# Row sums spread into the attention tile's free half, own slots for the down weights, an early Silu table and fewer warm-ups in a hybrid decoder layer

## The chip, the cores and the metric

One core of a Trainium2 chip runs the whole kernel, one launch. The metric is device time in microseconds (us), lower is better. The kernel before took 1362.46 us (median of 3 runs, 1359.22 to 1362.53). Engines: PE (TensorE), DVE (VectorE), ACT (ScalarE), POOL (GpSimd), SP (SyncE, which here only issues DMAs).

## What is computed

One decoder layer on 16 meta tokens and 1024 tokens of width 1024, in float32:

```python
u = rmsnorm(h, attn_norm_w)
proj = u @ w_in                       # split: gated-DeltaNet heads | forgetting-attention heads
o_gdn = gated_deltanet_group(...)     # 4 heads, chunked delta rule
o_fox = forgetting_attention_group(...)   # 8 heads of 64, softmax attention with a forget-gate bias
h = h + concat(o_gdn, o_fox) @ w_out
h = h + swiglu(rmsnorm(h, ffn_norm_w), w_gate, w_up, w_down)   # (silu(x@w_gate) * (x@w_up)) @ w_down
out = rmsnorm(h, final_norm_w)[16:]
```

The hidden width of the FFN is 2816, that is 22 blocks of 128.

## The kernel before

The stages follow each other on PE: projections and DeltaNet preparation (to about 300 us), scan and remaining projections, attention (to about 610 us), output projection and norm (to about 716 us), first FFN half (to about 1110 us), second FFN half. Every fp32 product is three matmuls: each operand is cut into a rounded high part (`split`, line 158, an ACT cast) and the rest (line 159, a DVE subtraction). In the FFN both products use seven products of sums of quarter blocks instead of eight products (a Strassen scheme, p1 to p7).

PE's order is written out by hand from the scan on (`manual_schedule`); the other engines and the SP queue are put in order by a scheduler that plays the program through with planned durations, so an edit anywhere can exchange neighbours in their queues. Each engine works through its queue in order, SP its DMAs too, and a tile's buffer can be written again only when its last readers are done.

**The attention part of the output projection.** `prep(tt)` (lines 1100 to 1109) readies one of eight token tiles; the order is 0, 4, 1, 5, 2, 6, 3, 7 (`ORDER`). It loads the unnormalised attention output from DRAM into `of` (128 x 8 x 128; the two halves hold the two parts of a split product, two buffers), POOL adds the halves into `of[:, 0:4]` (line 1104), `row_scale` (lines 1091 to 1097) has POOL spread the inverse row sums into a tile `rx` (line 1093), PE transposes `rx` into PSUM (`rbt`, line 1096), DVE multiplies (line 1106), and the product is split into `oh`, `ol`. The tile `rx` has no memory of its own: it lies in the slot `ub0_0`.

That slot belongs to `u_blocks` (lines 1171 to 1204), which transposes the normed tile `xn` (`u2t`, line 1178) and, for tiles 4 to 7, forms the sums for the Strassen scheme; `ub0_0` holds `b12` there, written at line 1196 and read at line 1199. So `rx` of a later tile can be written only after `u_blocks` of an earlier one has read `b12`. `out_fox` (lines 1156 to 1168) does the projection itself, 24 matmuls a tile (`wof`), the residual add on DVE (line 1162), the norm and a store.

**The first FFN half.** `ffn_in(j)` runs 11 pairs of hidden blocks. `w_ops` (lines 1218 to 1230) loads two gate blocks and two up blocks (`raw`, 512 KB each, DMA line 1215), DVE forms four sums for each of gate and up (lines 1223 to 1226), and ACT and DVE split them. `down_sums(j)` (lines 1240 to 1251) loads two blocks of `w_down` into tiles of the same tag `raw` (four buffers for six tiles a pair), POOL forms four sums (lines 1246 to 1249), and four DMAs write them to DRAM (line 1251, `wt_p`). Evictions on DVE are line 1282 (`gx`, `gz` and the like). The split of p1 and p2 of pair 0 is made early, in a pool `pf` (inside `if i == 3`), while the output projection still runs.

At the start 24 matmuls on a tile of ones (`WARM`, line 131) keep PE busy until the first transposes.

Of the kernel before, what the change touches and what calls it, by code (L numbers as in the profile page):

```python
# [9 lines left out]
F32 = mybir.dt.float32  # L10
F32R = mybir.dt.float32r
AF = mybir.ActivationFunctionType
ALU = mybir.AluOpType
# [23 lines left out]
CO = 3.0  # L37
RES = 6
ORDER = (0, 4, 1, 5, 2, 6, 3, 7)
WARM = 24  # L40


class PeOrder:
# [52 lines left out]
def tile_hymba_layer(ctx, tc, x, meta, attn_norm_w, w_in, conv_w, a_log, dt_bias, gdn_norm_w,  # L96
# [991 lines left out]
        turn[tag] = turn.get(tag, -1) + 1  # L1088
        return wo2.tile(shape, dt, tag=slot or f"{tag}_{turn[tag] % bufs}", name=f"{tag}_{nm}")

    def row_scale(tt):
        rx = wo_tile("rx", [P, 4, P], 1, tt, slot="ub0_0")
        G.tensor_copy(rx.rearrange("p m (i c) -> p (m i) c", i=2), rinv[:, :, tt:tt + 1].broadcast_to([P, FH, DH]))
        pt = ps_s(f"rbt_{tt}").rearrange("p (a b) -> p a b", a=4)
        for m in range(4):
            nc.tensor.transpose(pt[:, m], rx[:, m], ident)
        rbk[tt] = pt

    def prep(tt):
        cols = slice(P * tt, P * tt + P)  # L1100
        oh, ol = (wo_tile(t, [P, 4, P], 2, tt, F32R) for t in ("oh", "ol"))
        of = wo_tile("of", [P, 8, P], 2, tt)
        nc.sync.dma_start(of, o_d[:, :, :, cols].rearrange("i k p c -> p (i k) c"))
        G.tensor_tensor(of[:, 0:4], of[:, 0:4], of[:, 4:8], op=ALU.add)
        row_scale(tt)
        V.tensor_mul(of[:, 0:4], rbk[tt], of[:, 0:4])
        cast = split(oh, ol, of[:, 0:4])
        pre_u[tt] = (oh, ol)
        return cast

    def load_h(tt):
# [91 lines left out]
        put("p5", t1, G)  # L1203
        put("p4", t4, G)

    f1 = [None]
    wops = {(m, j): {} for m in "gu" for j in range(NF)}

    def w_split(m, j, p, src, pool, bufs):
        hi, lo = (pool.tile([P, H], F32R, tag=f"w{c}", bufs=bufs, name=f"w{c}_{m}{j}_{p}") for c in "hl")  # L1210
        split(hi, lo, src)
        wops[m, j][p] = (hi, lo)

    def w_raw(t, v, f):
        nc.sync.dma_start(t.rearrange("p (k c) -> p k c", k=KT), v[:, :, P * f:P * f + P])

    def w_ops(v, j, m):
        r0, r1 = (f1[0].tile([P, D], F32, tag="raw", bufs=4, name=f"raw_{m}{j}_{i}") for i in range(2))
        for r, f in ((r0, j), (r1, j + NF)):
            w_raw(r, v, f)  # L1220
        a11, a12, a21, a22 = r0[:, :H], r0[:, H:], r1[:, :H], r1[:, H:]
        s2, s3, s4 = (f1[0].tile([P, H], F32, tag=f"ws{i}", bufs=2, name=f"ws{i}_{m}{j}") for i in range(3))
        V.tensor_tensor(s3, a11, a21, op=ALU.subtract)  # L1223
        V.tensor_tensor(a21, a21, a22, op=ALU.add)
        V.tensor_tensor(s2, a21, a11, op=ALU.subtract)
        V.tensor_tensor(s4, a12, s2, op=ALU.subtract)
        for p, src in zip(ORD, (a11, s2, a12, s3, a21, a22, s4)):
            if p not in wops[m, j]:
                w_split(m, j, p, src, f1[0], 7)
            yield  # L1230

    def block3(dst, p, wop, first):
# [5 lines left out]
                                 stop=(k == 3 and i == 2), skip_group_check=not first)  # L1238

    def down_sums(j):  # L1240
        q0, q1 = (f1[0].tile([P, D], F32, tag="raw", bufs=4, name=f"raw_d{j}_{i}") for i in range(2))
        for q, f in ((q0, j), (q1, j + NF)):
            nc.sync.dma_start(q, w_down[P * f:P * f + P])
        b11, b12, b21, b22 = q0[:, :H], q0[:, H:], q1[:, :H], q1[:, H:]
        t3 = f1[0].tile([P, H], F32, tag="dt3", bufs=1, name=f"dt3_{j}")
        G.tensor_tensor(t3, b22, b12, op=ALU.subtract)
        G.tensor_tensor(b12, b12, b11, op=ALU.subtract)
        G.tensor_tensor(b22, b22, b12, op=ALU.subtract)
        G.tensor_tensor(b21, b21, b22, op=ALU.subtract)
        for p, t in (("p7", t3), ("p5", b12), ("p6", b22), ("p4", b21)):  # L1250
            nc.sync.dma_start(wt_d[p, j], t)
# [59 lines left out]
    with tc.manual_schedule(engines={mybir.EngineType.PE}):  # L1311
# [4 lines left out]
        for i, tt in enumerate(ORDER):  # L1316
            out_fox(tt, 0)
            if i >= 2:
                u_blocks(ORDER[i - 2])
            if i == NT - 1:  # L1320
                u_blocks(ORDER[i - 1])
            out_fox(tt, 1)
            if i + 2 < NT:
                prep(ORDER[i + 2])
                load_h(ORDER[i + 2])
            if i == 3:
                for m, v in (("g", w_g_v), ("u", w_u_v)):
                    r = wraw.tile([P, WMAX], F32, tag="raw", name=f"raw_{m}")[:, :D]
                    w_raw(r, v, 0)
                    for p, src in (("p1", r[:, :H]), ("p2", r[:, H:])):  # L1330
                        w_split(m, 0, p, src, pfp, 4)
        done = [("p1", "g"), ("p1", "u")]
        for p, m in done:
            sbs[m, 0] = {"x": pfp.tile([P, H], F32, name=f"{m}x0")}
# [150 lines left out]
```

## Time and profile before

| | |
|---|---|
| median of 3 runs (range) | 1362.46 us (1359.22 to 1362.53) |
| the profiled execution: its own time, its span | 1361.58 us, 1359.8 us |
| mean granted TensorE clock | 0.986 |
| PE busy | 1308.9 us, 96% of the span |
| DVE, ACT, POOL busy | 859.9, 543.6, 424.0 us |
| HBM traffic | 177 GB/s over the span |

The span runs from the first to the last instruction; the execution's own time is 1.8 us longer. Busy PE time counts a matmul from start to end, also while the granted clock is halved: the share of the full clock has to be read beside it. In rows of the timeline the first number is the start in us from the span's beginning, the second the duration, and brackets hold the idle time of the engine before the instruction and what ended it.

### The profile page before, as it was taken

The page shows a single profiled execution, that of the slowest core. Times are in us where ns is not written, and L with a number is a line of the kernel's source. Part 1 is how long each engine was busy: PE and PEld are TensorE (multiplying, and loading weights), DVE is VectorE, ACT ScalarE, POOL GpSimd, SP SyncE. Part 2 cuts the span into 40 slices and gives each one's busy share as a digit, 9 for nine tenths or more (in the row PEclk, how much of TensorE's full clock was granted, in tenths as well). Part 3 has the DMA queues.
Part 4 walks back from the last instruction along what each step waited for, and adds up shares of the span by engine and source line. Part 5 has one row for each costly group of instructions (what it writes and reads, how often), then busy time and mean ns, then how long its engine had stood idle before and what let it go on. Part 6 is the DMA issues. An engine that isn't in the chain of part 4 may idle for free.

```text
span 1359.8 us, 20162 instructions
## 1 busy us (share of the span) xinstructions
PE 1308.9 (96%) x7417; PEld 1137.2 (84%) x7417; DVE 859.9 (63%) x1505; ACT 543.6 (40%) x914; POOL 424.0 (31%) x422
## 2 busy tenths in 40 slices
PE   8999999999999899999778999999999999999997
PEld 7999999899999778887566878787888888888876
DVE  6565779657446578985677556666555566455653
ACT  6443543222223467872353233222223334333341
POOL 3111123211112256742432444433444443010300
PEclk9999999899999999999898999999999999999998
DMA  8131465784397898836526544445455556965522
GB/s 291 65 91 47 141 178 162 205 229 140 126 314 244 206 260 245 219 98 200 171 93 178 178 152 147 141 155 162 142 170 178 163 179 233 402 246 182 214 84 93
DMA packets 196201, 242.11 MB, mean 178 GB/s; under 512 B 18944, under 2 KB 146808, under 8 KB 192264
## 3 DMA queue, kind: packets, MB, share of 16 engines
q1 hardware_dynamic: 196104, 240.84, 56.6%
q8 instruction: 58, 0.95, 0.3%
q14 instruction: 39, 0.32, 0.1%
HBM read 161.62 MB, written 79.18 MB: 177 GB/s over the span
## 4 chain that ended last, share of the span: by engine, by line
PE 56%; DMA 15%; DVE 14%; POOL 7%; issue 5%; SPq 1%; ACT 1%; DVEq 0%; POOLq 0%; ACTq 0%
PE xp L1395 8%; PE yp L1395 6%; DMA raw_u<-in_w_up_dram 5%; PE pj_fk L199 3%; PE pj_fq L199 3%; DMA wt_p<-raw_d 3%; DMA raw_d<-in_w_down_dram 2%; PE wog L199 2%; PE pt L961 2%; DVE wl_u_p L159 2%; PE po L982 1%; PE pj_k L190 1%; PE pj_k L189 1%; PE pj_v L191 1%; PE pj_q L191 1%
## 5 line engine op out<-in xcount | busy, mean ns | idle before, releaser
L159 DVE TENSOR_TENSOR al_p<-ra_p,ah_p 128x2048 fp32r<-128x2048 f32 (+1 forms) x21 | 46.8, 2230 | 92.5 <-ACT ah_p L158 92.5
L914 POOL TENSOR_TENSOR bi<-ccol,cr 128x144 f32<-128x144 f32 (+7 forms) x60 | 70.7, 1182 | 55.5 <-DVE sm L930 51.2
L158 ACT CAST ah_p<-ra_p 128x2048 fp32r<-128x2048 f32 (+1 forms) x21 | 37.1, 1765 | 103.7 <-PE yp L1395 44.4
L1287 POOL TENSOR_TENSOR gz<-gz,uz 128x512 f32<-128x512 f32 x11 | 18.3, 1665 | 178.9 <-DVE uz L1282 149.8
L1395 PE MATMUL xp<-wl_p,ah_p 128*128 128x512 f32 x176 | 69.3, 394 | 1.8 <-DVE wl_p L159 1.8
L1395 PE MATMUL xp<-wh_p,al_p 128*128 128x512 f32 x176 | 69.1, 393 | 0.0
L1395 PE MATMUL xp<-wh_p,ah_p 128*128 128x512 f32 x176 | 69.0, 392 | 0.0
L158 ACT CAST wh_u_p<-raw_u 128x512 fp32r<-128x512 f32 x44 | 27.2, 620 | 74.6 <-DMA raw_u<-in_w_up_dram 23.7
L159 DVE TENSOR_TENSOR wl_u_p<-raw_u,wh_u_p 128x512 fp32r<-128x512 f32 x44 | 47.0, 1069 | 15.4 <-ACT wh_u_p L158 15.4
L935 ACT ACTIVATE pr<-pr,sm 128x144 f32<-128x144 f32 (+3 forms) x64 | 50.6, 791 | 13.7 <-DVE sm L930 12.1
L159 DVE TENSOR_TENSOR pl<-pt,ph 128x512 fp32r<-128x512 f32 (+1 forms) x96 | 51.5, 552 | 5.1 <-ACT ph L158 4.7
L159 DVE TENSOR_TENSOR wl_g_p<-raw_g,wh_g_p 128x512 fp32r<-128x512 f32 x44 | 38.7, 881 | 23.4 <-ACT wh_g_p L158 23.4
L158 ACT CAST ph<-pt 128x512 fp32r<-128x512 f32 (+1 forms) x96 | 45.2, 473 | 20.3 <-PE pt L961 18.3
L158 ACT CAST wh_g_p<-raw_g 128x512 fp32r<-128x512 f32 x44 | 27.1, 619 | 63.7 <-PE ub L1237 42.0
L1223 DVE TENSOR_TENSOR ws_g<-raw_g,raw_g 128x512 f32<-128x512 f32 x11 | 7.6, 692 | 69.6 <-DMA raw_g<-in_w_gate_dram 69.6
L1395 PE MATMUL yp<-wh_p,ah_p 128*128 128x512 f32 x132 | 51.3, 389 | 0.0
L1395 PE MATMUL yp<-wl_p,ah_p 128*128 128x512 f32 x132 | 51.3, 389 | 0.0
L1395 PE MATMUL yp<-wh_p,al_p 128*128 128x512 f32 x132 | 51.3, 389 | 0.0
L159 DVE TENSOR_TENSOR wl_p<-rw_p,wh_p 128x2048 fp32r<-128x2048 f32 (+1 forms) x21 | 46.5, 2213 | 4.7 <-ACT wh_p L158 4.7
L961 PE MATMUL pt<-ident,pr 128*128 128x128 f32 x288 | 48.2, 276 | 0.0
L927 PE MATMUL sc<-kk,sa 128*128 128x144 f32 (+6 forms) x112 | 40.7, 364 | 4.9 <-issue 3.3
L930 DVE CUSTOM_DVE_ANT_0 pr<-sc,bi 128x144 f32<-128x144 f32 (+3 forms) x64 | 31.5, 492 | 15.7 <-PE sc L928 11.8
(591 smaller groups left out, 4521.7 us busy)
## 6 DMA issues: line engine op xcount, KB each, us to landing
ra_p<-ao_p SPq DMA_DIRECT2D x14, 1024.0 KB, 6.4
raw_g<-in_w_gate_dram SPq DMA_DIRECT2D x23, 512.0 KB, 4.8
raw_u<-in_w_up_dram SPq DMA_DIRECT2D x23, 512.0 KB, 5.4
raw_d<-in_w_down_dram SPq DMA_DIRECT2D x22, 512.0 KB, 4.6
wt_p<-raw_d SPq DMA_DIRECT2D x33, 256.0 KB, 2.4
kk<-k_d SPq DMA_DIRECT2D x16, 520.0 KB, 10.0
rw_p<-wt_p SPq DMA_DIRECT2D x8, 1024.0 KB, 6.1
rw_p<-in_w_down_dram SPq DMA_DIRECT2D x6, 1024.0 KB
```

The source lines that it names most:

```text
L158: cast = nc.scalar.copy(dst_hi, src)
L159: nc.vector.tensor_sub(dst_lo, src, dst_hi.bitcast(F32))
L189: nc.tensor.matmul(dst, lh, rh, start=(i == 0), stop=False)
L191: nc.tensor.matmul(dst, ll, rh, start=False, stop=(i == n - 1))
L199: nc.tensor.matmul(dst, a, b, start=first, stop=last)
L914: nc.gpsimd.tensor_tensor(bi[:, :n], ccol[:, h, j:j + 1].broadcast_to([P, n]), cr[:, :n], op=ALU.subtract)
L927: nc.tensor.matmul(sc[:, :b - a], sa[:, q0:q0 + P], kk[:, 0, a:b], start=True, stop=False)
L930: V.tensor_tensor_reduce(out=pr[:, a:b], in0=sc[:, :b - a], in1=bi[:, a:b], scale=1.0, scalar=3e38 if i == 0 else sm[:, i - 1:i], op0=ALU. ...
L935: nc.scalar.activation(pr[:, :n], pr[:, :n], AF.Exp, bias=sm[:, np_ - 1:np_], scale=-1.0, accum_out=rsum[:, h, j:j + 1])
L961: nc.tensor.transpose(pt[:rows_k, P * j:P * j + P], pts[j][0][:, c0:c0 + rows_k], ident)
L1287: G.tensor_tensor(gs[d], gs[d], us[d], op=ALU.mult)
L1395: nc.tensor.matmul(dst, a[:, f, c], b[:, f], start=(first and i == 0 and n == 0), stop=(i == NF - 1 and n == 2), skip_group_check=cont)
```

## The change

- `rx` goes. `row_scale(tt, rx)` now gets `of[:, 4:8]`, the half of the attention tile that is free once POOL has added it into the other one.
- Ten tiles of the output projection's pool are laid out first, so that their places are known.
- The two `w_down` tiles of a pair get four slots of their own, in the pool `pf` (`pf0` to `pf3`, used by turns), and not the four `raw` buffers; their loads are issued after the pair's last `w_up` load (`tc.issue_after`). The early splits of pair 0 share those slots.
- For pair 0, `w_ops` forms the two sums that p6 needs first, in another order, and is stepped once before the loop over the pairs.
- A one-element Silu activation is put in the output projection (`sil`, line 1344 of the changed kernel), which brings the load of ACT's Silu table there.
- 20 warm-up matmuls and not 24.

```diff
-WARM = 24
+WARM = 20
-    def row_scale(tt):
-        rx = wo_tile("rx", [P, 4, P], 1, tt, slot="ub0_0")
+    def row_scale(tt, rx):
         G.tensor_copy(rx.rearrange("p m (i c) -> p (m i) c", i=2), rinv[:, :, tt:tt + 1].broadcast_to([P, FH, DH]))
...
-        row_scale(tt)
+        row_scale(tt, of[:, 4:8])
...
+    for tag in ("of_0", "of_1", "oh_0", "ol_0", "oh_1", "ol_1", "hst_0", "xn2_0", "hst_1", "xn2_1"):
+        big = tag[:2] in ("hs", "xn")
+        wo2.tile([P, D] if big else [P, 8 if tag[1] == "f" else 4, P], F32R if tag[1] in "hl" else F32, tag=tag,
+                 name=f"lay_{tag}")
...
+    def pf_tile(i, nm, dt=F32R):
+        return pfp.tile([P, D], F32R, tag=f"pf{i}", name=nm)
...
+        if not j:
+            V.tensor_tensor(s3, a21, a22, op=ALU.add)
+            V.tensor_tensor(s2, s3, a11, op=ALU.subtract)
+            w_split(m, j, "p6", s2)
+            yield
+            V.tensor_tensor(s4, a12, s2, op=ALU.subtract)
+            V.tensor_tensor(a11, a11, a21, op=ALU.subtract)
+            srcs = (None, s2, None, a11, s3, a22, s4)
...
-        q0, q1 = (f1[0].tile([P, D], F32, tag="raw", bufs=4, name=f"raw_d{j}_{i}") for i in range(2))
-        for q, f in ((q0, j), (q1, j + NF)):
-            nc.sync.dma_start(q, w_down[P * f:P * f + P])
+        q0, q1 = (pf_tile(2 * (j % 2) + i, f"raw_d{j}_{i}").bitcast(F32) for i in range(2))
+        with tc.issue_after(raw_dma["u", j].ins):
+            for q, f in ((q0, j), (q1, j + NF)):
+                nc.sync.dma_start(q, w_down[P * f:P * f + P])
...
             if i == 3:
+                nc.scalar.activation(wo2.tile([P, 1], F32, name="sil"), mhalf[:, 0:1], AF.Silu)
...
         gens = {m: w_ops(v, 0, m) for m, v in (("g", w_g_v), ("u", w_u_v))}
+        for m in "gu":
+            next(gens[m])
```

PE's order is the same but for the four warm-ups. What moves stands in the queues of the others. On ACT, where attention ends and the output projection begins (`oa` holds the last attention output on its way to DRAM, `ph` a transposed block of the last head), there stood before:

```order
L158 CAST ph_7_6_7425<-pt_7_6_7422 128x256
L158 CAST ph_7_7_7433<-pt_7_7_7431 128x128
L986 COPY oa_7_7443<-po_7_7377 128x512
L158 CAST oh_7500<-of_7502 128x512
L158 CAST oh_7515<-of_7517 128x512
```

and now:

```order
L158 CAST ph_7_6_7421<-pt_7_6_7418 128x256
L158 CAST ph_7_7_7429<-pt_7_7_7427 128x128
L1344 ACT_TABLE_LOAD
L1344 ACTIVATE sil<-mhalf 128x1
L986 COPY oa_7_7439<-po_7_7373 128x512
L158 CAST oh_7506<-of_7508 128x512
L158 CAST oh_7520<-of_7522 128x512
```

The table load and the small activation stand ahead of the last copy of attention. On POOL, in the prep of all eight tiles (`of` the attention tiles, `rx` the spread row sums, `st_f` a norm's power, `br` and `ul_p` the work of `u_blocks`), there stood before:

```order
L1093 COPY rx_7505<-rinv 128x512
L1104 TENSOR_TENSOR of_7502<-of_7502 128x512
L1093 COPY rx_7520<-rinv 128x512
L1104 TENSOR_TENSOR of_7517<-of_7517 128x512
...
L1104 TENSOR_TENSOR of_8005<-of_8005 128x512
L1201 TENSOR_TENSOR br_0_7805<-br_0_7805,ub_4_7875 128x512
L1184 TENSOR_TENSOR ul_p_7650<-br_0_7804,uh_p_7649 128x4x128
L1093 COPY rx_7918<-rinv 128x512
```

and now:

```order
L1103 TENSOR_TENSOR of_7508<-of_7508 128x512
L1092 COPY of_7508<-rinv 128x512
L1103 TENSOR_TENSOR of_7522<-of_7522 128x512
L1092 COPY of_7522<-rinv 128x512
...
L1103 TENSOR_TENSOR of_7916<-of_7916 128x512
L1092 COPY of_7916<-rinv 128x512
L205 TENSOR_TENSOR st_f_7908<-st_f_7908,mhalf 128x1
L1103 TENSOR_TENSOR of_8003<-of_8003 128x512
L1204 TENSOR_TENSOR br_0_7807<-br_0_7807,ub_4_7876 128x512
L1187 TENSOR_TENSOR ul_p_7654<-br_0_7806,uh_p_7653 128x4x128
L1092 COPY of_8003<-rinv 128x512
```

Each copy now follows the add of its own tile (the first pair of rows is tile 0, the second tile 4); that of tile 6 (`of_7916`) moved ahead of the work of `u_blocks`, that of tile 3 (`of_8003`) stands two instructions behind its add. On SP, in one pair of the first FFN half (`raw_g`, `raw_u`, `raw_d` loads of gate, up and down weights, `ao_p` stores of activations, `wt_p` stores of the down sums), there stood before:

```order
L1243 DMA raw_d_0_9158<-in_w_down_dram 128x1024
L1298 DMA ao_p_7610<-gx_8589 128x512
L1243 DMA raw_d_1_9159<-in_w_down_dram 128x1024
...
L1251 DMA wt_p_7634<-raw_d_1_9159 128x512
L1215 DMA raw_g_1_9172<-in_w_gate_dram 128x8x128
L1298 DMA ao_p_7622<-uz_8660 128x512
L1215 DMA raw_u_0_9201<-in_w_up_dram 128x8x128
L1215 DMA raw_u_1_9202<-in_w_up_dram 128x8x128
```

and now:

```order
L1260 DMA raw_d_0_9154<-in_w_down_dram 128x1024
L1260 DMA raw_d_1_9155<-in_w_down_dram 128x1024
...
L1268 DMA wt_p_7638<-raw_d_1_9155 128x512
L1315 DMA ao_p_7623<-gz_8635 128x512
L1221 DMA raw_g_0_9167<-in_w_gate_dram 128x8x128
...
L1221 DMA raw_u_0_9197<-in_w_up_dram 128x8x128
L1221 DMA raw_u_1_9198<-in_w_up_dram 128x8x128
L1260 DMA raw_d_0_9459<-in_w_down_dram 128x1024
L1260 DMA raw_d_1_9460<-in_w_down_dram 128x1024
```

The down loads now stand directly behind the up loads, ahead of the pair's stores, and no longer in turn with them.

## Rows read from the trace of the kernel before

**Rows 1.** Who waited for whom on PE, the whole span (total, times, longest).

```profile
PE rbt L1096 <- POOL rx L1093: 15.1, 3, 9.3
PE gd L1237 <- DVE gz L1282: 4.9, 6, 1.8
...
PE u2t L1178 <- DVE xn L1040: 1.8, 2, 1.2
```

**Rows 2.** Busy time by stage: output projection and norm (PE, PEld, DVE, ACT, POOL, clock, DMA).

```profile
640.00:728.00 88.00, 65.89 (x295) 52.03 (x294) 64.81 (x91) 40.99 (x75) 31.45 (x28) 0.88 0.45 144
```

**Rows 3.** Timeline of PE at the waits of that stage.

```profile
617.29 0.66 PE L1096 MATMUL rbt<-ident,rx 128*128 128x128 f32 x4 [0.80 <-POOL rx L1093]
...
648.83 0.60 PE L1096 MATMUL rbt<-ident,rx 128*128 128x128 f32 x4
...
665.71 1.12 PE L1096 MATMUL rbt<-ident,rx 128*128 128x128 f32 x4 [9.27 <-POOL rx L1093]
...
674.34 0.60 PE L1096 MATMUL rbt<-ident,rx 128*128 128x128 f32 x4
...
686.42 1.11 PE L1096 MATMUL rbt<-ident,rx 128*128 128x128 f32 x4 [5.07 <-POOL rx L1093]
...
720.65 0.80 PE L1237 MATMUL gb<-uh_p,wh_g_p 128*128 128x512 f32 x1 [3.56 <-ACT wh_g_p L158]
```

**Rows 4.** Busy time and clock after the waits of 5.07 and 3.56 us.

```profile
686.00:690.00 4.00, 3.58 (x11) 3.00 (x12) 2.89 (x2) 0.12 (x1) 2.12 (x3) 0.57 0.00 0
721.00:727.00 6.00, 5.45 (x13) 3.76 (x13) 5.79 (x10) 3.23 (x7) 0.00 (x0) 0.50 0.54 173
```

**Rows 5.** Timeline of POOL in the prep of tile 4.

```profile
616.63 0.61 POOL L1093 COPY rx<-rinv 128x512 f32<-128x512 f32 x1 [2.34 <-PE rbt L1096]
619.26 1.29 POOL L1104 TENSOR_TENSOR of<-of 128x512 f32<-128x512 f32 x1 [2.02 <-DMA of<-o_d]
```

**Rows 6.** Timeline of ACT and SP at the end of attention.

```profile
609.49 0.27 ACT L158 CAST ph<-pt 128x128 fp32r<-128x128 f32 x1 [0.22 <-PE pt L961]
610.50 0.59 ACT L986 COPY oa<-po 128x512 f32<-128x512 f32 x1 [0.74 <-PE po L982]
...
614.88 0.38 SPq L1103 DMA_DIRECT2D of<-o_d  x1
```

**Rows 7.** Timeline of ACT and DVE at the first pair's sums.

```profile
715.10 1.28 ACT L1277 ACT_TABLE_LOAD   x1
716.39 0.60 ACT L1277 ACTIVATE gw<-ga 128x512 f32<-128x512 f32 x1
...
717.20 0.69 DVE L1279 TENSOR_TENSOR gw<-ua,gw 128x512 f32<-128x512 f32 x1 [0.82 <-PE ua L1237]
```

**Rows 8.** Timeline of SP and POOL in the prep of tile 3.

```profile
656.17 0.37 SPq L1103 DMA_DIRECT2D of<-o_d  x1
...
660.51 1.71 POOL L1104 TENSOR_TENSOR of<-of 128x512 f32<-128x512 f32 x1 [4.77 <-DVE hst L1162]
662.18 1.71 POOL L1201 TENSOR_TENSOR br<-br,ub 128x512 f32<-128x512 f32 x1
663.85 1.26 POOL L1184 TENSOR_TENSOR ul_p<-br,uh_p 128x512 fp32r<-128x512 f32 x1
```

**Rows 9.** Chain of waits in one pair of the first FFN half (start, length).

```profile
846.67 3.76 DMA wt_p<-raw_d
...
850.97 7.29 DMA raw_u<-in_w_up_dram
...
863.19 0.60 DVE gz L1282
```

**Rows 10.** Timeline of PE and POOL at the start.

```profile
1.19 8.48 PE L131 MATMUL warm<-ones 128*128 128x128 f32 x48 [1.19 <-POOL ones L128]
...
13.14 1.02 POOL L322 TENSOR_TENSOR nea<-euler,gsm 128x4 f32<-128x4 f32 x1 [6.74 <-DMA gsm<-in_a_log_dram]
...
16.04 1.09 PE L239 MATMUL pt_a<-ident,xn_a 128*128 128x128 f32 x8 [0.83 <-DVE xn_a L232]
```

More of the change, by code (lines that the diff above doesn't have):

```diff
@@ L1204, in u_blocks, with w_split @@
         put("p4", t4, G)
-    f1 = [None]
+    f1, raw_dma = [None], {}
     wops = {(m, j): {} for m in "gu" for j in range(NF)}
-    def w_split(m, j, p, src, pool, bufs):
-        hi, lo = (pool.tile([P, H], F32R, tag=f"w{c}", bufs=bufs, name=f"w{c}_{m}{j}_{p}") for c in "hl")
+    def w_split(m, j, p, src, hl=None):
+        hi, lo = hl or (f1[0].tile([P, H], F32R, tag=f"w{c}", bufs=7, name=f"w{c}_{m}{j}_{p}") for c in "hl")
         split(hi, lo, src)
         wops[m, j][p] = (hi, lo)
+    def pf_tile(i, nm, dt=F32R):
+        return pfp.tile([P, D], F32R, tag=f"pf{i}", name=nm)
     def w_raw(t, v, f):
-        nc.sync.dma_start(t.rearrange("p (k c) -> p k c", k=KT), v[:, :, P * f:P * f + P])
+        return nc.sync.dma_start(t.rearrange("p (k c) -> p k c", k=KT), v[:, :, P * f:P * f + P])
     def w_ops(v, j, m):
@@ L1219, in w_ops @@
         for r, f in ((r0, j), (r1, j + NF)):
-            w_raw(r, v, f)
+            raw_dma[m, j] = w_raw(r, v, f)
         a11, a12, a21, a22 = r0[:, :H], r0[:, H:], r1[:, :H], r1[:, H:]
         s2, s3, s4 = (f1[0].tile([P, H], F32, tag=f"ws{i}", bufs=2, name=f"ws{i}_{m}{j}") for i in range(3))
[L1223 to L1227, printed above, removed]
+        if not j:
[6 more added lines that the diff above has]
+            srcs = (None, s2, None, a11, s3, a22, s4)
+        else:
+            V.tensor_tensor(s3, a11, a21, op=ALU.subtract)
+            V.tensor_tensor(a21, a21, a22, op=ALU.add)
+            V.tensor_tensor(s2, a21, a11, op=ALU.subtract)
+            V.tensor_tensor(s4, a12, s2, op=ALU.subtract)
+            srcs = (a11, s2, a12, s3, a21, a22, s4)
+        for p, src in zip(ORD, srcs):
             if p not in wops[m, j]:
-                w_split(m, j, p, src, f1[0], 7)
+                w_split(m, j, p, src)
             yield
@@ L1329, in tile_hymba_layer @@
                     w_raw(r, v, 0)
-                    for p, src in (("p1", r[:, :H]), ("p2", r[:, H:])):
-                        w_split(m, 0, p, src, pfp, 4)
+                    hi, lo = (pf_tile(2 * "gu".index(m) + i, f"w{c}_{m}0") for i, c in enumerate("hl"))
+                    for p, c in (("p1", slice(0, H)), ("p2", slice(H, D))):
+                        w_split(m, 0, p, r[:, c], (hi[:, c], lo[:, c]))
         done = [("p1", "g"), ("p1", "u")]
```

## The prediction, made before the changed kernel had run

> **What bounds the kernel now.** The page's engine table comes first: PE is busy for 1308.9 of 1359.8 us, so only time in which PE stands still, or runs at half clock, can be won. The view of who waits for whom on PE then names the waits that this change can touch [rows 1]: 15.1 us in three waits of the transposes `rbt` for `rx`, 4.9 us in six waits of `gd` for DVE's `gz` (the first FFN half), 1.8 us in two waits for `xn`. The timeline of PE places the first ones [rows 3]: 0.80 at tile 4, 9.27 at tile 6, 5.07 at tile 7, and 3.56 at the first `gb` of the FFN, which waits for ACT's split `wh_g_p`. The granted clock stands at 0.57 of full, so near the lower level of 1.2 GHz for most of the stretch, after the 5.07 us wait, and at 0.50 after the 3.56 us one [rows 4]. A long wait here is followed by slow matmuls, which the waits view does not count. In the same stage DVE is busy for 64.81 of 88 us and POOL for 31.45 [rows 2]: DVE is the engine that will stand behind PE once `rx` is out of the way.
>
> Why the `rbt` waits are there: `rx` lies in the slot of `b12`, so POOL may spread the row sums of a later tile only after `u_blocks` of an earlier one has read `b12`. In the FFN, the chain of one pair shows [rows 9] that the `raw_u` load starts at 850.97, when the store `wt_p` (846.67 + 3.76 = 850.43) has read the buffer it wants, takes 7.29, and DVE's `gz` at 863.19 is late by what is left.
>
> **The change part by part.** All sums are against the profiled execution (1361.58, span 1359.8); the median of the runs is 0.9 above it.
>
> *Removed: the `rbt` waits, -15.1* [rows 1, 3]. The spread sums no longer need the slot of `b12`; they go into the tile's own `of`, as soon as POOL has added its halves. *The slow stretch after the 5.07 wait, -1.7*: 4.0 us at 0.57 give 4.0 x (1 - 0.57) [rows 4]. The stretch after the 9.27 wait I count at nothing: what it lost was taken from the wait at tile 7, whose input did not hang on PE.
>
> *Removed: the loop's waits, -4.9* [rows 1]. With slots of their own, the down weights release `raw_u` from the store. The load then waits only for DVE's sums of the pair before, which are several us earlier than the 850.43 of [rows 9]; the longest of the six waits is 1.8. The store keeps its length, but nothing on PE's path waits for it. The early splits of pair 0 now share these slots, so pair 0's down load waits for PE's last use of p1 and p2; nobody waits for down sums before the second half.
>
> *First pair's sums, -0.7*: p6 now needs two DVE sums where three stood ahead of its split; one such 128x512 operation takes 0.69 [rows 7]. `gw` still stands first on DVE, so the wait of 3.56 shrinks to 2.9 and does not go. Together -22.4.
>
> *Added: tile 4's chain, +4.6.* The copy of the row sums could be made at any time before; now it stands behind its own tile's DMA and add. Tile 4's `of` load is issued at 614.88 [rows 6], its add begins 4.38 later at 619.26 and takes 1.29, the copy 0.61 [rows 5]. That ends at 621.15, and `rbt` of tile 4 began at 617.29 [rows 3]: +3.85, on top of the 0.80 that is counted as removed. The table load adds to it. It begins behind the last `ph` cast, at 609.49 + 0.27 = 609.76, takes 1.28 [rows 6, 7], and the small activation some 0.2 (estimate, a third of the 0.60 of a full `gw`), so `oa` starts at 611.25 and not at 610.50: +0.75, since `oa`'s store goes ahead of the load of `of`. A wait of some 5 us stands beside the 5.07 that was followed by slow matmuls: *+1.7* [rows 4].
>
> *Added: tile 3, +2.4.* From `rbt` of tile 2 (648.83) to the issue of tile 3's load is 7.34, to its add 4.34 more [rows 3, 8]; add, two pieces of `u_blocks` that now stand between, and copy take 1.71 + 1.71 + 1.26 + 0.61 [rows 5, 8]. That makes 16.9. PE's own work between the two transposes is 674.34 - 648.83 = 25.5, less the wait of 9.27 and the slow stretch of about 1.7: 14.5. The wait is 2.4, at least 0 (if the add goes ahead by 2.4 without the 4.77 it waited) and at most 3.4 (if POOL is later by the 1.0 that one more piece of its queue costs).
>
> *Added: DVE comes out, +2.5.* With 15 us gone from 88, the 64.81 us of DVE work stand in 73. The nearest waits on DVE there are the two for `xn`, 1.8 in all [rows 1]. Below: 0, if DVE's slack is spread evenly. Above: 5, if each of the four tiles with Strassen sums waits as long as the longest of them, 1.2. I take the middle, as the share of DVE rises to nearly nine tenths. *One more slow stretch, +1.7*, since tile 3's wait or the first `gb` can be long enough for it, the one of 3.56 stood with 0.50 behind it [rows 3, 4]; bounds 0 and 3.4 (two of them). Together +12.9.
>
> *At nothing.* The table load where it was, at 715.10 [rows 7]: DVE's `gw` waited 0.82 for PE's `ua` after it, so PE hid it; if PE were earlier there, up to 1.28 would be won. The warm-ups: 24 take 8.48 at the start, so four take 1.4, but the transposes at 16.04 hang on other work (POOL is held until 13.14 by a load), so they end in time that was idle [rows 10]; bounds 0 and, if the clock falls before the transposes, half of their first 1.09. The order of layout tiles and of SP's loads issues nothing more.
>
> The page ScalarE: Activation LUTs of the Trainium skill, section "What ACT_TABLE_LOAD costs", speaks against putting the load in that place: a switch is 1283 ns of load and about 1380 ns of drain. The load's 1.28 agrees [rows 7]; a drain does not show, as `gw` begins at 716.39, just when the load ends. By that rule the sum would be 1.4 less of a gain.
>
> Sum: -22.4 + 12.9 = **-9.5**. Span 1350.3, execution 1352.1, median **1353.0**. With the three bounded terms (2.4, 2.5, 1.7) at their ends, 0 and 11.8, the added part is 6.3 to 18.1, the median 1346.4 to 1358.2.
>
> **The rivals.** A difference within 0.3% of the time, 4.1 us, is about what a measurement of this kernel cannot tell from none.
>
> *The table load holds ACT longer.* In this kernel nothing follows the old load but `gw`, so a stop inside ACT after the small activation could be unseen. As long again as the load itself, 1.28, it would move `oa` and tile 4 by that much: -8.2, 1354.2. For it: the place is new, and it is on the path. Against: `gw` starts at the old load's end [rows 7]. 0.07. By the rule above it would be 1354.4; the trace so far bears out the load alone.
>
> *The loop's waits stay.* The load of `raw_u` takes 7.29 [rows 9] and shares the DMA engines with the down loads that now stand directly behind it; if those slow it as much as it starts earlier, the 4.9 remain: -4.6, 1357.9. 0.12, half of it within 0.3%.
>
> *All cover holds.* DVE has room, tile 3 is in time, no second slow stretch: +6.3 only, 1346.4. For it: no wait for DVE in this stage is over 1.2 [rows 1]. Against: these waits were measured with PE held back by 15 us. 0.13.
>
> *The gain comes back on DVE whole.* The 15.1 turn into waits for `xn` and for the products of the row sums: -22.4 + 6.3 + 15.1 = -1.0, 1361.5, no change. For it: 64.81 of 88 [rows 2]. Against: 73 is still more than 64.81. 0.08.
>
> *Slower: the chain of tile 4 repeats at each tile.* Load, add and copy stand one behind the other for all eight tiles (4.38 + 1.29 + 0.61), and each load waits for the buffer of the tile two before. If the six later tiles wait, the sum turns when they total 22.4 - 6.3 = 16.1, 2.7 each. At 3.56 each, the wait of the one late split here [rows 3], it is 21.4: +5.3, 1367.8. Against it: tile 3's load, as late as any, gives 2.4, and it has two foreign pieces before its copy. 0.05.
>
> **How the numbers follow.** The forecast, 1353.0, has 0.55. The range goes from 1346.0, under the case with all cover, to 1359.0, above the loop's waits staying; outside it are the case of no change, the slower one and some of the loop's (about 0.17). Faster by over 0.3% (under 1358.4): 0.55 + 0.07 + 0.13 + half of 0.12 = 0.81. Within: 0.08 + 0.06 = 0.14. Slower: 0.05.
>
> **What would show it right or wrong.** In the profile after, the waits of `rbt` at tiles 6 and 7 are gone; one wait of about 5 us stands at tile 4, about 617 to 622, with POOL's copy into `of` as what ended it, and a halved clock behind it; tile 3 waits 2 to 3; the first `gb` about 2.9; no `gd` waits for `gz`; a `raw_u` load starts at DVE's last read and not at a store. Two or more tiles of the output projection waiting over 3 us each besides tile 4, `gd` still waiting for `gz`, or `xn` waits of over 5 us in all would make the prediction wrong.

## The result, and the profile after

The changed kernel takes 1352.66 us (median of 4 runs, 1351.02 to 1354.89), beside 1362.49 of the kernel before: a ratio of 0.9935, interval 0.9913 to 0.9957, so 5.9 to 11.9 us faster. Forecast were 1353.0 us, in a range of 1346.0 to 1359.0. The profiled execution took 1351.02 us, its span is 1349.1.

Who waited for whom on PE, changed kernel (total, times, longest):

```profile
PE rbt L1095 <- POOL of L1092: 9.7, 3, 4.9
...
PE u2t L1181 <- DVE xn L1040: 3.9, 2, 2.9
...
PE gb L1253 <- ACT wh_g_p L158: 2.8, 1, 2.8
...
PE ub L1253 <- DVE uy L1299: 1.0, 1, 1.0
```

Against [rows 1], `rbt` went from 15.1 to 9.7 us, and its waits are others. `gd` no longer waits for `gz`. `xn` doubled.

Timeline of PE, changed kernel: the first `wog` of the output projection, the tiles' `rbt` (the 1st row is tile 0, the 2nd tile 4, then tiles 1, 6, 3 and 7), a `u2t`, the first `gb`, and a matmul of pairs 0 and 8:

```profile
612.40 0.45 PE L199 MATMUL wog<-whi_wo,ogh 128*128 128x512 f32 x1
...
621.19 1.11 PE L1095 MATMUL rbt<-ident,of 128*128 128x128 f32 x4 [3.03 <-POOL of L1092]
627.24 1.11 PE L1095 MATMUL rbt<-ident,of 128*128 128x128 f32 x4 [4.94 <-POOL of L1092]
...
646.30 0.60 PE L1095 MATMUL rbt<-ident,of 128*128 128x128 f32 x4
...
666.15 0.60 PE L1095 MATMUL rbt<-ident,of 128*128 128x128 f32 x4
...
674.97 0.66 PE L1095 MATMUL rbt<-ident,of 128*128 128x128 f32 x4 [1.73 <-POOL of L1092]
...
682.02 0.66 PE L1095 MATMUL rbt<-ident,of 128*128 128x128 f32 x4
...
685.31 1.03 PE L1181 MATMUL u2t<-ident,xn 128*128 128x128 f32 x8
...
717.31 0.79 PE L1253 MATMUL gb<-uh_p,wh_g_p 128*128 128x512 f32 x1 [2.83 <-ACT wh_g_p L158]
...
730.53 0.47 PE L1253 MATMUL ub<-uh_p,wh_u_p 128*128 128x512 f32 x1 [0.98 <-DVE uy L1299]
...
1048.88 0.39 PE L1253 MATMUL gd<-uh_p,wh_g_p 128*128 128x512 f32 x1
```

The same instructions of the kernel before, where [rows 3] do not have them:

```profile
610.30 0.45 PE L199 MATMUL wog<-whi_wo,ogh 128*128 128x512 f32 x1
...
634.40 0.60 PE L1096 MATMUL rbt<-ident,rx 128*128 128x128 f32 x4
...
691.28 1.04 PE L1178 MATMUL u2t<-ident,xn 128*128 128x128 f32 x8
...
732.62 0.39 PE L1237 MATMUL ub<-uh_p,wh_u_p 128*128 128x512 f32 x1
...
1057.68 0.47 PE L1237 MATMUL gd<-uh_p,wh_g_p 128*128 128x512 f32 x1 [0.15 <-DVE gz L1282]
```

PE's order is the same in both kernels, so the differences between equal instructions, start to start, say where the time went:

| stretch of PE | difference at its end | in the stretch | forecast |
|---|---|---|---|
| to the first `wog` (610.30, 612.40) | +2.1 | +2.1 | 0 |
| tiles 0 and 4, to `rbt` of tile 1 (634.40, 646.30) | +11.9 | +9.8 | +5.5 |
| tiles 1 to 7, to the `u2t` behind tile 7 (691.28, 685.31) | -6.0 | -17.9 | -13.6 |
| to the first pair's second `ub` (732.62, 730.53) | -2.1 | +3.9 | +3.5 |
| the loop, to `gd` of pair 8 (1057.68, 1048.88) | -8.8 | -6.7 | -4.9 |
| the rest, to the end of the span | -10.7 | -1.9 | 0 |

(The forecast's 5.5 is 4.6 + 1.7 - 0.8; its -13.6 is -9.27 - 5.07 - 1.7 + 2.4; its 3.5 is 2.5 + 1.7 - 0.7.) The total was met by terms that were off on both sides: that they cancel so well is luck.

The clock stood low after tiles 0 and 4 in the changed kernel, and after tiles 6 and 7 in the kernel before. Busy time by stage (length, PE, PEld, DVE, ACT, POOL, clock, DMA share, GB/s), changed kernel:

```profile
610.00:640.00 30.00, 22.03 (x94) 17.55 (x93) 8.38 (x13) 4.94 (x10) 7.89 (x8) 0.83 0.58 178
640.00:690.00 50.00, 47.87 (x238) 38.68 (x236) 40.37 (x59) 25.35 (x46) 18.90 (x19) 1.00 0.58 188
```

Kernel before:

```profile
610.00:640.00 30.00, 29.20 (x134) 23.77 (x134) 12.61 (x19) 5.96 (x9) 6.94 (x7) 1.00 0.70 218
640.00:690.00 50.00, 34.25 (x158) 27.25 (x157) 36.13 (x50) 20.38 (x39) 21.82 (x20) 0.86 0.47 153
```

### The profile page after: what moved, and what is told of

Same layout as the page of the kernel before. It is cut to its first block, busy times and chain, and to the rows that moved or that the text cites. A ratio compares the mean times of both kernels' runs of the same rounds, so it can differ in the third digit from the quotient of the medians.

```text
span 1349.1 us, 20148 instructions
## 1 busy us (share of the span) xinstructions
PE 1305.0 (97%) x7409; PEld 1136.4 (84%) x7409; DVE 890.9 (66%) x1505; ACT 549.2 (41%) x915; POOL 429.3 (32%) x422
## 4 chain that ended last, share of the span: by engine, by line
PE 75%; DMA 10%; DVE 9%; issue 3%; SPq 1%; ACT 1%; POOL 1%; DVEq 0%; POOLq 0%; ACTq 0%
PE xp L1416 8%; PE yp L1416 6%; PE ud L1253 4%; PE gd L1253 4%; PE ub L1253 4%; PE ga L1253 4%; PE ua L1253 4%; PE gb L1253 4%; PE pj_fk L199 3%; PE pj_fq L199 3%; PE ue L1253 2%; PE ge L1253 2%; PE pt L961 2%; PE wog L199 1%; DMA rkr<-rk_d 1%
## 5 line engine op out<-in xcount | busy, mean ns | idle before, releaser
L1263 POOL TENSOR_TENSOR dt<-raw_d,raw_d 128x512 f32<-128x512 f32 x11 | 17.8, 1621 | 140.2 <-issue 80.7
L935 ACT ACTIVATE pr<-pr,sm 128x144 f32<-128x144 f32 (+3 forms) x64 | 50.6, 791 | 16.4 <-DVE sm L930 15.1
L159 DVE TENSOR_TENSOR wl_u_p<-raw_u,wh_u_p 128x512 fp32r<-128x512 f32 x42 | 35.2, 837 | 13.5 <-ACT wh_u_p L158 13.5
L158 ACT CAST wh_u_p<-ws_u 128x512 fp32r<-128x512 f32 x33 | 20.5, 622 | 56.5 <-PE gb L1253 21.9
L1416 PEld LDWEIGHTS xp<-wl_p,ah_p 128*128 128x128 f32 x176 | 33.0, 188 | 9.1 <-DVE wl_p L159 2.2
```

The source lines that it names most:

```text
L158: cast = nc.scalar.copy(dst_hi, src)
L159: nc.vector.tensor_sub(dst_lo, src, dst_hi.bitcast(F32))
L935: nc.scalar.activation(pr[:, :n], pr[:, :n], AF.Exp, bias=sm[:, np_ - 1:np_], scale=-1.0, accum_out=rsum[:, h, j:j + 1])
L1416: nc.tensor.matmul(dst, a[:, f, c], b[:, f], start=(first and i == 0 and n == 0), stop=(i == NF - 1 and n == 2), skip_group_check=cont)
```

## The experiments

All ratios are against the kernel before. The last column is the profiled execution's time from the first `wog` to the end of the span (749.5 in the kernel before: 1359.8 - 610.30). It comes from one profile of each kernel. It leaves out the stages ahead of it, which differ in the warm-ups alone and yet are scattered: the first `wog` of the changed kernel and of its 12 relatives here starts anywhere from 608.15 to 614.39 us, and at 608.15 and 612.45 in two profiles of one program (e4, e11). And it holds some 1.7 us of low clock behind one wait late in the span, in the kernel before, e2, e5 and e6 but in none of the others (shown further below).

| kernel | median us | ratio | interval | from `wog` |
|---|---|---|---|---|
| the change | 1352.66 | 0.9935 | 0.9913 to 0.9957 | 736.7 |
| the change again (e10) | 1350.18 | 0.9919 | 0.9900 to 0.9937 | 736.5 |
| e1, two row sums early | 1343.85 | 0.9879 | 0.9852 to 0.9906 | 732.8 |
| e2, no layout | 1351.18 | 0.9933 | 0.9909 to 0.9957 | 737.3 |
| e3, no early Silu | 1351.99 | 0.9935 | 0.9912 to 0.9958 | 736.6 |
| e4, 24 warm-ups | 1348.81 | 0.9928 | 0.9902 to 0.9953 | 738.8 |
| e11, e4 again | 1350.07 | 0.9922 | 0.9898 to 0.9946 | 736.9 |
| e5, down tiles back | 1356.77 | 0.9975 | 0.9956 to 0.9993 | 743.9 |
| e6, row sums back | 1357.42 | 0.9986 | 0.9972 to 1.0001 | 745.7 |
| e7, e1 and 24 warm-ups | 1340.55 | 0.9860 | 0.9837 to 0.9883 | 728.9 |
| e8, the program of e7 | 1341.88 | 0.9870 | 0.9849 to 0.9891 | 728.4 |
| e9, e7 and late down sums | 1338.39 | 0.9830 | 0.9809 to 0.9852 | 726.9 |
| e12, e9 without early Silu | 1338.56 | 0.9840 | 0.9818 to 0.9863 | 726.3 |

### Why tiles 0 and 4 wait: e1, e2, e3

e1, the copy of these two tiles ahead of the add and in tiles of their own:

```diff
+        rx = wo_tile("rx", [P, 4, P], 1, tt, slot=f"ub{tt // 4}_0") if tt in ORDER[:2] else of[:, 4:8]
+        if tt in ORDER[:2]:
+            row_scale(tt, rx)
         G.tensor_tensor(of[:, 0:4], of[:, 0:4], of[:, 4:8], op=ALU.add)
-        row_scale(tt, of[:, 4:8])
+        if tt not in ORDER[:2]:
+            row_scale(tt, rx)
```

> The changed kernel, but tiles 0 and 4 spread their row sums into tiles of their own (in the slots ub0_0 and ub1_0, which nothing uses yet), ahead of their adds. Theory 1 (in the changed kernel these two copies wait for their own attention tile's load, which costs PE 3.03 + 4.94 us and some 2.5 us of half clock behind them): both rbt waits go, the clock stays full from 610 to 640 us, the first wof does not wait, as 48 wog matmuls stand before it: 8 to 10.5 us less than the changed kernel, 1342 to 1345 us. Rival (the wait only moves: the same late load then holds the first wof): both rbt waits go, but a wait of 3 us or more stands at the first wof of tiles 0 or 4: less than 5 us won, 1348 us or more.

Timeline of PE, e1 (tiles 0 and 4 in one row; tile 1; a `gb` of the first pair):

```profile
614.84 1.04 PE L1095 MATMUL rbt<-ident,rx 128*128 128x128 f32 x8
...
632.40 0.60 PE L1095 MATMUL rbt<-ident,of 128*128 128x128 f32 x4
...
719.20 0.76 PE L1257 MATMUL gb<-uh_p,wh_g_p 128*128 128x512 f32 x1 [3.17 <-DVE gy L1303]
```

Theory 1 holds: no wait at either tile, and tile 1 comes 23.2 us behind the first `wog` (609.23) where the change needed 33.9: 10.7 us won there. Against the change itself the ratio fell by 0.0056 (7.6 us of 1360.77), a little less than the 8 to 10.5 expected; against e10 it fell by 0.0040 (5.4 us), and there the intervals overlap. A part of the 10.7 came back: 6.3 are left at the first `gb` of the first pair (707.81, against 717.31 in the change) and 3.9 at its second `ub`, since from the one to the other e1 needs 15.7 us where the change needs 13.2. There `gb` now waits 3.17 us for DVE.

e2:

```diff
-    for tag in ("of_0", "of_1", "oh_0", "ol_0", "oh_1", "ol_1", "hst_0", "xn2_0", "hst_1", "xn2_1"):
...
```

> The changed kernel without the ten tiles that are laid out first. Theory 2 (the layout puts the norm weights and the attention tile of tile 0 on memory that attention's last casts still use, so their loads start 3.2 and 1.8 us later against the end of attention than before, and the last attention store queues behind 1.5 MB of loads): the load of the norm weights starts 3 us or more ahead of the last cast, tile 0's rbt waits less than 1 us in place of 3.03, tile 4's about 3 in place of 4.94: 4 to 5 us less than the changed kernel, 1347.5 to 1349 us. Rival (the waits are the price of the copy behind the add alone, wherever the tiles lie): the two waits stay within 1 us of 8 in sum, and so does the time, 1352 to 1354 us.

Timeline of SP: loads of the norm weights (`nwb`) and of the attention tile of tile 0, the last attention store, the load of tile 4's. Kernel before:

```profile
606.27 0.53 SPq L1117 DMA_DIRECT2D nwb<-in_ffn_norm_w_dram  x1
608.23 0.37 SPq L1103 DMA_DIRECT2D of<-o_d  x1
...
611.11 1.09 SPq L989 DMA_DIRECT2D o_d<-oa  x2
```

The change:

```profile
611.59 0.36 SPq L1120 DMA_DIRECT2D nwb<-in_ffn_norm_w_dram  x1
612.15 0.81 SPq L1102 DMA_DIRECT2D of<-o_d  x1
...
613.93 1.27 SPq L989 DMA_DIRECT2D o_d<-oa  x2
...
620.96 0.38 SPq L1102 DMA_DIRECT2D of<-o_d  x1
```

e2:

```profile
607.56 0.52 SPq L1116 DMA_DIRECT2D nwb<-in_ffn_norm_w_dram  x1
609.50 0.37 SPq L1102 DMA_DIRECT2D of<-o_d  x1
...
613.06 1.09 SPq L989 DMA_DIRECT2D o_d<-oa  x2
...
617.20 0.38 SPq L1102 DMA_DIRECT2D of<-o_d  x1
```

Against the first `wog` (611.59 in e2), the `nwb` load starts 4.03 us early before and in e2, and 0.81 early in the change; the first `of` load 2.07, 2.09 and 0.25 early. So the layout is what delays both. Tile 4's `of` load starts 5.6 us behind the first `wog` in e2, 8.6 in the change: the last attention store that it needs stood behind three loads of 512 KB there, and landed 6.6 us after its issue, not 3.4 as before. In e2 tile 0 does not wait, tile 4 waits 5.53 us, more than the 3 expected because PE is there sooner, and tile 1 comes 30.7 us behind the first `wog`: the layout costs 3.2 us up to there. But the time did not follow: `gb` of the first pair waits 3.19 us for `gy`, as in e1, and 1.2 of the 3.2 us are left at the second `ub`; the low clock late in the span, which the change's profile does not have, took the rest. So theory 2 was right about the place and wrong about the time.

e3:

```diff
-                nc.scalar.activation(wo2.tile([P, 1], F32, name="sil"), mhalf[:, 0:1], AF.Silu)
```

> The changed kernel without the one-element Silu activation: the table load returns to the first gw. Theory (the load stands in the way of the last attention copy for 1.4 us, of which 0.75 reach tile 4, and was hidden at its old place): tile 4 waits 0.7 to 1.4 less, gw's table load costs nothing: 1351.5 to 1352.3 us. Rival A (the load at its old place now holds gw, and so the first gb, as PE is earlier there): gb waits up to 1.3 longer, 1352.7 to 1353.5 us. Rival B (a table switch holds ACT for longer than its 1.28 us): tile 4 waits over 2 us less, 1350 us or less.

Timeline of ACT, the change:

```profile
611.88 1.28 ACT L1344 ACT_TABLE_LOAD   x1
613.17 0.20 ACT L1344 ACTIVATE sil<-mhalf 128x1 f32<-128x1 f32 x1
613.28 0.57 ACT L986 COPY oa<-po 128x512 f32<-128x512 f32 x1
```

The time is in the theory's range, but its mechanism is not there: tiles 0 and 4 wait 1.87 and 6.28 us, 8.15 in all and not less than the 7.97 of the change. The load does not reach PE: SP issues the last attention store 1.47 us behind the first `wog` in e3 (611.86 against 610.39) and 1.53 behind it in the change, since the late loads stand ahead of it in SP's queue. At its old place the load is hidden too: `gb` waits 2.83 in both. Nothing is gained or lost.

### What the two main parts are worth: e5, e6

e5:

```diff
-        q0, q1 = (pf_tile(2 * (j % 2) + i, f"raw_d{j}_{i}").bitcast(F32) for i in range(2))
-        with tc.issue_after(raw_dma["u", j].ins):
-            for q, f in ((q0, j), (q1, j + NF)):
-                nc.sync.dma_start(q, w_down[P * f:P * f + P])
+        q0, q1 = (f1[0].tile([P, D], F32, tag="raw", bufs=4, name=f"raw_d{j}_{i}") for i in range(2))
+        for q, f in ((q0, j), (q1, j + NF)):
+            nc.sync.dma_start(q, w_down[P * f:P * f + P])
```

> The changed kernel with the two down tiles of a pair back in the four buffers of the gate and up tiles, and their loads back at their old place in SP's queue. Theory 1 (the own slots are what took the waits out of the first FFN half): gd waits for gz again, 5 to 7 us from 732 to 1100 us (the changed kernel went from 2.1 to 8.8 us ahead of the kernel before there); against it, POOL's first down sums start later and leave DVE alone at the first pair, up to 1.4: 1357 to 1359 us. Rival (the order of the first pair's sums, or DVE's earlier start, took them out): no wait for gz over 0.5 us, 1352 to 1354 us.

Who waited for whom on PE, e5:

```profile
PE gd L1253 <- DVE gz L1298: 5.4, 6, 1.9
```

The six waits are back, and from the first `wog` on the kernel takes 7.2 us more than the change, 1.7 of them at the low clock late in the span; the ratio rose by 0.0040 (5.4 us; the median is just under the 1357 to 1359 expected). The edit takes back the own slots and the loads' place in SP's queue together, so the two together are the cause. That no `gd` waits for `gz` in e9 either (below), which has the own slots and other places for the loads, speaks for the slots; the place alone was not tried.

e6:

```diff
-        row_scale(tt, of[:, 4:8])
+        row_scale(tt, wo_tile("rx", [P, 4, P], 1, tt, slot="ub0_0"))
```

> The changed kernel with the row sums back in a tile that shares the slot ub0_0. Theory 2 (by the offsets of the two traces this part of the change gave 17.9 us at tiles 1 to 7 and took 9.8 at tiles 0 and 4): waits of 9 and 5 us stand at tiles 6 and 7 again, tiles 0 and 4 wait less than 1.5 us, the time rises by about 8: 1359 to 1362 us. Rival (DVE is the bound of this stage, and would have been as late without these waits): the rbt waits return, but the waits for xn, ol and gy shrink by as much: 1353 to 1356 us.

Timeline of PE, e6, tiles 6 and 7:

```profile
668.34 1.12 PE L1095 MATMUL rbt<-ident,rx 128*128 128x128 f32 x4 [9.12 <-POOL rx L1092]
...
688.72 1.11 PE L1095 MATMUL rbt<-ident,rx 128*128 128x128 f32 x4 [3.58 <-POOL rx L1092]
```

The waits are back, so the slot is their cause: 9.0 us more from the first `wog` on (1.7 of them at the low clock late in the span), 6.9 by the ratio. The median, 1357.42, lies between the two ranges, and a part of the rival is there: the waits for `xn` fell from 3.9 to 1.7 us and that for `ol` (1.54) is gone. Tile 4 waits 1.62, a little over the 1.5 expected.

### The warm-ups: e4, e10, e11, e7

e4 and e11 have one edit; e10 is the change itself.

```diff
-WARM = 20
+WARM = 24
```

> The changed kernel with 24 warm-up matmuls. Theory (the last four ended in idle time, but without them the clock fell to half under the first transposes, which left the changed kernel 0.2 to 0.4 us later at 21 us; the 1.8 us that it was later still at 234 us is the run's own scatter): the first transposes run at full clock; 1352.3 us, not to be told from the changed kernel. Rival (the fewer warm-ups are the cause of the 2.1 us that the changed kernel is late when attention ends): 2 us less, 1350.6 us, and the waits of pq for kq back at 3.2 us.

> The changed kernel as it is, beside e11 on the same chip, to tell what four warm-ups are worth. Theory (nothing): 1351 to 1353.5 us, the clock of the first 21 us at 0.92 or 1.00 as it falls, and e11 within 1.5 us of it. Rival (the last four warm-ups are worth 3 us): e11 is 2 us or more faster.

> e4 once more (the changed kernel with 24 warm-ups), beside e10. Theory (nothing): within 1.5 us of e10. Rival: 2 us or more under e10, as e4 was under e2 and e3.

e4 looked some 3 us faster than e2 and e3, which were measured with it; beside each other on one chip, e10 and e11 are 0.1 us apart. Nothing can be told between 20 and 24.

e7 is e1 with `WARM = 24`:

> As e1 (the row sums of tiles 0 and 4 early and in tiles of their own), with 24 warm-up matmuls. Theory (the warm-ups are worth nothing that can be measured; e4's 3 us against e2 and e3 was scatter of the stages ahead of attention): 1343 to 1345 us, the same as e1. Rival (the last four warm-ups keep the clock up under the first transposes, and the stages behind them stay ahead by some 3 us): 1340 to 1342 us, and attention ends no later than 609 us.

Its median is in the rival's range, but not by the rival's cause: the first `wog` starts at 609.21, as in e1 (609.23). The intervals of e1 and e7 overlap. The profile of e7 differs from e1's behind `wog`, at the first pair (waits of 0.42 and 1.02 for 3.17; 13.2 us from the first `gb` to the second `ub` for 15.7), where the warm-ups are 700 us past. What differs there is when POOL's first down sum starts: 3.7 us behind the first `gb` in e1 and 4.9 in e7. DVE's splits that start beside it and stand ahead of `gy` take 1.75 to 1.78 us each, four of them in e1 and two in e7 (the next part shows what they wait for).

### What DVE waits for at the first pair: e8, e9, e12

In the change, POOL and DVE at the first pair. DVE (`wl` splits, and `gy`, an eviction from PSUM):

```profile
721.72 0.68 DVE L159 TENSOR_TENSOR wl_g_p<-raw_g,wh_g_p 128x512 fp32r<-128x512 f32 x1
722.32 1.78 DVE L159 TENSOR_TENSOR wl_u_p<-raw_u,wh_u_p 128x512 fp32r<-128x512 f32 x1
724.02 1.77 DVE L159 TENSOR_TENSOR wl_g_p<-ws_g,wh_g_p 128x512 fp32r<-128x512 f32 x1
725.72 0.68 DVE L1299 TENSOR_TENSOR gy<-gb,gx 128x512 f32<-128x512 f32 x1
```

POOL (the first down sums):

```profile
722.01 1.54 POOL L1263 TENSOR_TENSOR dt<-raw_d,raw_d 128x512 f32<-128x512 f32 x1 [6.81 <-DMA raw_d<-in_w_down_dram]
723.63 1.62 POOL L1264 TENSOR_TENSOR raw_d<-raw_d 128x512 f32<-128x512 f32 x1
725.33 1.61 POOL L1265 TENSOR_TENSOR raw_d<-raw_d,raw_d 128x512 f32<-128x512 f32 x1
```

A split of the same size takes 0.68 when it starts ahead of POOL's first sum (721.72 against 722.01) and 1.78 when it starts behind it: it ends 0.55 us behind POOL's instruction (724.10 against 723.55), which is nearly its own length. The eviction, with one operand in PSUM, keeps its 0.68 in the middle of a POOL sum. In the kernel before POOL's sums began at 728.24, behind most of the first pair's splits.

e8 called the down sums one pair later:

```diff
-            down_sums(j)
+            if j:
+                down_sums(j - 1)
+        down_sums(NF - 1)
```

> As e7, with the down sums of each pair made one pair later. Theory 3 (the own slots let POOL's first down sums start while DVE splits the first pair's operands, and the two stretch each other: splits of 1.78 us in place of 0.69, so that gb waits 3.2 us for gy): the splits at the first pair take 0.69, the wait of gb for gy falls under 0.5 us: 2 to 3 us less than e7. Rival (the splits are long because ACT and the loads are at work, POOL's sums only happen to stand beside them): the splits stay at 1.7 us and the wait at 3 us; the same time as e7. What could go wrong for both: the last pair's sums and stores come late for the second half, and its first products wait for rw_p.

It moved no instruction: the loads and sums stand in every queue where e7 has them. So it says nothing of theory 3, and its 1341.88 is e7's kernel measured once more. e9 has e8's edit, and holds the loads back as well:

```diff
-        with tc.issue_after(raw_dma["u", j].ins):
+        with tc.issue_after(raw_dma["u", min(j + 1, NF - 1)].ins):
```

> As e7, but the down loads of a pair are issued behind the up loads of the next pair, so that POOL's down sums come one pair later (e8's edit moved nothing in any queue, so it was e7 once more). Theory 3 (POOL's first down sums and DVE's splits of the first pair stretch each other): POOL sums nothing from 704 to 722 us, all splits there take 0.69, the first wait of ub for uy (1.0 in e7, 2.1 in e8) and of gb for wh_g_p (0.4 in e7, beside the 2.8) go: 1 to 2 us less than e7 and e8, 1339 to 1340.5 us. Rival (something else stretches the splits): splits of 1.7 us remain, same time as e7, 1340.5 to 1342 us.

Timeline of POOL and DVE at the same place, e9:

```profile
723.70 1.60 POOL L1267 TENSOR_TENSOR dt<-raw_d,raw_d 128x512 f32<-128x512 f32 x1 [19.28 <-PE gd L1257]
```

```profile
711.53 0.68 DVE L159 TENSOR_TENSOR wl_u_p<-raw_u,wh_u_p 128x512 fp32r<-128x512 f32 x1
...
714.54 0.68 DVE L159 TENSOR_TENSOR wl_u_p<-raw_u,wh_u_p 128x512 fp32r<-128x512 f32 x1
...
724.08 1.78 DVE L1244 TENSOR_TENSOR ws_u<-raw_u,raw_u 128x512 f32<-128x512 f32 x1
```

Busy time in e9 while the last splits of that group run (columns as above):

```profile
713.00:716.00 3.00, 3.00 (x15) 2.48 (x14) 2.74 (x5) 0.77 (x2) 0.00 (x0) 1.00 1.08 296
```

All splits there take 0.68, and after the first `gb` (2.83, as before) PE waits nowhere in the pair. e9 moves the down loads too, but the rival does not stand: from 713 to 716 us the DMA engines are full (a share of 1.08) and the splits keep their 0.68, and the 1.78 moved along with POOL, to the first DVE sum that starts beside POOL's (724.08). That shows the mechanism; e9 does not end the contention, it puts it where PE waits for none of it. From the first `gb` to the second `ub` of the pair the change needs 13.2 us, and so do seven more of the traces whose POOL sums stand beside the splits (e7 and e8 among them); e9 needs 11.5, e12 10.6, and e5, where the sums come late as well, 10.7.

From the first `wog` on e9 takes 1.5 and 2.0 us less than e8 and e7. The median fell to 1338.39, under the range expected (1339 to 1340.5), but the intervals of e7 and e9 overlap. e9 has the lowest median of the study: a ratio of 0.983, 0.9809 to 0.9852.

e12 is e9 with e3's edit:

> As e9 without the one-element Silu activation. Theory (with the row sums of tiles 0 and 4 early, nothing waits behind the early table load, and at its old place it would hold the first gw, which now is nearer to the path): gb waits up to 1.3 longer, 0.5 to 1.3 us more than e9. Rival (the load is hidden at either place): the same as e9 within 0.3 us.

The same within what can be measured; `gw` starts at 704.04 behind its table load, and the `gb` wait is 2.83 in both, with 0.55 more behind it in e12 only. The load is hidden at either place, as the rival said.

## Why the prediction was right, and where it was not

**The `rbt` waits of tiles 6 and 7** went, as forecast; the slot `ub0_0` was their cause (e6). **The loop's waits** went with the shared buffers and the old place of the loads (e5); 4.9 was too small for what they cost: 6.7 between the traces.

**Tile 4's chain, +4.6,** is borne out by e2, where the loads are in their old places: `rbt` of tile 4 starts at 623.60, 12.0 us behind the first `wog`; the steps gave 7.0 + 4.6 = 11.6. What failed is "The order of layout tiles and of SP's loads issues nothing more". True of instructions, but a place in memory has a last reader, and by the times of the loads attention used the new places of `nwb` and `of` to its end (which tiles of it was not tried). The loads came 3.2 and 1.8 us later, just ahead of the attention store. So tile 0 waited as well (3.03), which the prediction did not have, and the two tiles took 9.8 us, not 5.5. The 0.75 for the table load, a part of the 4.6, was hidden in the change behind the late loads (e3). What the 9.8 hold beyond the waits (3.03 + 4.94 - 0.80) is 2.6, at a clock of 0.57 from 620 to 632 us; 1.7 was forecast for it.

**The slow stretch after the 9.27 wait, "at nothing",** was the error on the other side. From tile 6 to tile 3 the kernel before took 8.63 us [rows 3], the changed one 8.82 with a wait of 1.73 in it, so 7.09 of work: the slow clock had cost 1.54. It was no part of the wait at tile 7: that wait would have been longer by as much without it, so both go together. Small waits of the kernel before that went too (for `oh`, `ol` and `br`, 0.89, 0.16 and 0.37) were not counted either.

**Tile 3, +2.4,** was 1.73 in the change and 2.11 in e10, within its bounds. **DVE, +2.5:** waits of 1.54 for `ol`, 2.85 and 1.08 for `xn`, against 1.8 before; some 3.5 us more, within the bounds. The first `gb` waits 2.83, 2.9 forecast. **One more slow stretch, +1.7,** did not come: behind tile 3's wait the clock stayed at 1.00 (the row of 640 to 690 above), and the low clock behind the first `gb` (0.50 from 717 to 722) had been there before [rows 4].

**"Nobody waits for down sums before the second half"** is true and missed the point: the own slots let the loads, and POOL's sums, go first, beside DVE's splits (e9). It cost 1.4 us of waits in the change (0.39 and 0.98), and in e1 and e2, whose first pair takes 15.7 and 15.6 us for the change's 13.2, it gave back 2.4 of what they had won.

**The table load.** The page ScalarE: Activation LUTs of the Trainium skill ("What ACT_TABLE_LOAD costs") adds a drain of about 1380 ns to the load. Here the small activation starts at 613.17, 1.29 us behind the load's start, and the copy behind it at 613.28: no drain shows. That rival falls, and e3 shows that even the load costs nothing that can be measured here.

**The other rivals.** The loop's waits did not stay, and the cover did not hold whole. DVE gave back a part: e1 won 10.7 us at tile 1 and 3.9 at the end of its trace. The chain did not repeat at the later tiles: of them only tile 3 waits.

**What was not forecast and is not the change:** the 2.1 us ahead of the output projection lie within the scatter (608.15 to 614.39 in the 14 traces). Of the 1.9 us in the rest, most stand behind one wait that both kernels have. Kernel before, the wait and the stretch behind it:

```profile
1326.72 0.50 PE L1395 MATMUL xp<-wl_p,ah_p 128*128 128x512 f32 x1 [1.79 <-DVE wl_p L159]
```

```profile
1328.00:1332.00 4.00, 4.00 (x12) 3.16 (x11) 2.65 (x4) 1.15 (x2) 0.00 (x0) 0.57 0.61 245
```

The change:

```profile
1317.62 0.50 PE L1416 MATMUL xp<-wl_p,ah_p 128*128 128x512 f32 x1 [1.80 <-DVE st_o L204]
```

```profile
1318.00:1330.00 12.00, 12.00 (x54) 9.91 (x53) 5.37 (x7) 2.30 (x4) 1.76 (x4) 1.00 0.33 132
```

A wait of 1.79 was followed by 0.57 of the clock, one of 1.80 by the full clock. 4.0 x (1 - 0.57) = 1.7 us of difference. All 14 traces have this wait (1.72 to 1.80). Over the 8 us from its matmul on the clock is 0.79 in the kernel before, e2, e5 and e6 and 1.00 in the ten others, which is the 1.7 us named in the experiments. No edit touches this place; why those four fell is open.

Still open: whether e9's lead over e7 is all due to the splits (1.7 of the 2.0 us between the traces stand in the first pair, but the intervals overlap), why POOL's first down sum starts sooner in e1 than in e7, and whether the layout is worth undoing together with e9, which was not tried.

## What to carry to other kernels

A wait that is taken away lets the next engine start sooner: ask what that one will then run beside. Here freed buffers brought POOL's sums next to DVE's splits. A change in the order of tiles in a pool moves no instruction and still moves loads, because each place has a last reader; look up who that is before it is costed at nothing. And a slow stretch behind a removed wait goes with the wait, also where a later wait seems to have absorbed it.

## What the runs showed of the hardware

A DVE subtraction of two SBUF operands of 128x512 took 0.68 us alone and 1.78 beside POOL's sums, while a DVE eviction with one operand in PSUM kept 0.68. The page SBUF — State Buffer of the Trainium skill, section "SBUF: two separate sides", states a lock: such a DVE operation and a POOL one that reads SBUF use the same port pair, and the one that comes second waits for the whole of the first. The trace agrees: the stretched split ends 0.55 us behind POOL's sum, and the next POOL sum ends at 725.25 and the next split at 725.79.

The clock after a short wait is not settled by the wait's length (1.79 and 1.80 us above). In the first 21 us it stood at 0.92 or 1.00 in profiles with 20 warm-ups (0.92 in e10, 1.00 in e3) and with 24 (1.00 in e11, 0.92 in e7).
